# Attention's keys turned in one step, its units placed by other numbers, and the third gate group moved ahead of the branch projections

## The chip, the cores and the metric

The kernel runs on one core of one Trainium2 chip. The metric is the device time of one execution in microseconds (us). Before the change it was 1309.54 us, the median of 3 runs (1308.44 to 1310.19).

## The reference, cut to what matters

The program is a two-layer decoder trunk on 512 tokens of width 1024, all in float32. Each layer has a mixer (one wide input projection, a branch of windowed attention, a branch of mLSTM, gates, output projection) and a squared-ReLU MLP. The change is in the mixer:

```python
h = rmsnorm(x, norm_mix)
z = h @ w_in
q_a, k_a, v_a, q_m, k_m, v_m, o_m, if_m, gates = jnp.split(z, splits, axis=-1)
q_a = partial_rope(rmsnorm(q_a.reshape(B, S, 8, 64), att_q_norm), cos, sin)
k_a = partial_rope(rmsnorm(k_a.reshape(B, S, 2, 64), att_k_norm), cos, sin)
att = sliding_window_attention(q_a, k_a, v_a, att_sinks)      # blocks of 128, own and previous block
hm = mlstm_chunkwise(q_m, k_m, v_m, i_pre, f_pre)
hm = rmsnorm(hm, m_head_norm) * jax.nn.sigmoid(o_m)
g_a, g_m = jnp.split(gates, 2, axis=-1)
mixed = jax.nn.sigmoid(g_a) * (att @ w_att_branch) + jax.nn.sigmoid(g_m) * (hm @ w_m_branch)
x = x + mixed @ w_out
```

## The kernel before

**Matmuls.** TensorE (PE) works on float32 values that are split into a high part and a low rest (`wh`, `wl` for weights, `i` and others for activations), and every product is made of three matmuls (`mm3`, line 211). A *group* of the mixer is 512 output columns: 8 weight chunks of 128 x 512, each loaded by a DMA from SP's queue, split by ScalarE (ACT, line 192) and VectorE (DVE, line 193), and used by 4 x 3 = 12 matmuls of 128x512. These 12 matmuls are a *block*, the unit in which the program counts its own progress; a group is 8 blocks, 96 matmuls. A group's results leave PSUM by its own evictions.

**The order of the work.** `weave` (line 254) runs a list of such steps, the *fill*, each 0.25 blocks wide, and puts *side* steps between them when the fill has come to the block number that stands with them. Tile's scheduler then orders the instructions of each engine by priority, readiness by its own model and free buffers; the engines run their queues in order. The mixer's first weave makes attention's q, k, v and the gate logits. The second, in which the change lies, has nine groups as fill (line 865): mLSTM's q and k (blocks 0 to 8), gate groups 0 and 1 (to 24), mLSTM's v (to 32), the two halves of attention's branch projection (`a_steps`, to 48), gate group 2 (to 56), the o gate (to 64), gate group 3 (to 72).

**Attention in the second weave.** There are eight *units*, a unit being a block of 128 queries and one of the two key heads with its four query heads. Ahead of them stands the *rotation*: `k_vec(b)` and `q_vec(b)` (lines 585 and 602) normalise the keys or queries of token block b on DVE (line 570) and rotate 16 of the 64 dimensions by four GpSimd (POOL) instructions (lines 573 to 578). The *turn*: `k_tr(b)` and `q_tr(b)` transpose them on PE into an `aux` PSUM tile and evict that by ACT and DVE in pieces of 64 partitions (lines 597 to 600 for keys, 619 and 620 for queries). A unit then has `att_scores` twice (PE, then ACT line 642 and DVE line 643, which evict and mask), `att_softmax` (DVE lines 650 to 661, ACT line 656 for the exponentials), `att_probs` (PE transposes, ACT 204 and DVE 205 as eviction, POOL lines 675 and 677 as masks), and `att_out` (PE, then lines 689 to 697). Unit i is placed at block 7 + 1.65 i, its last step 5.65 blocks later.

**The aux tiles.** Everything on PE that is not a group's matmul writes an `aux` tile, of which there are two in PSUM. PE takes its instructions in order, so a PE instruction that needs an aux tile not yet evicted, or data not yet made, holds up the fill matmuls behind it.

**mLSTM in the second weave.** Its four heads start at block 28, 4.65 blocks apart: `m_decay`, four `m_weights` (exponentials on ACT lines 793 and 796, mask on POOL, product on DVE line 804) and four `m_out` (lines 806 to 817); `m_norm` stands at the end. Sigmoids of the gates (`sigmoid`, line 728) need another function table of ACT than the exponentials; `back` (line 733) loads the old one again. The gate groups 0 and 1 are gated after group 1, group 2 in the o gate's eviction (line 843).

## Time and profile before

| | |
|---|---|
| median of 3 runs | 1309.54 us |
| the profiled execution | 1309.28 us, its span 1307.5 us |
| PE busy | 1291.7 us, 99% of the span |
| DVE, ACT, POOL busy | 966.6, 780.2, 219.0 us |
| second weave, up to the first turn, layer 1 / layer 2 | from 46.5 / from 694.3 us |
| attention's units | 60.7 to 163.3 us / 708.5 to 811.2 us |
| mLSTM and after, to the weave's end | to 263 us / to 911 us |

The span is the time from the first to the last instruction; 1.78 us of the execution lie around it. All times in the trace count from the span's start. A row of the timeline has start, duration, engine, line, operation, output<-inputs and a count of merged instructions, and in brackets the idle time before it with what ended it. PE's matmuls are pipelined, so that a row's end is not the time at which the next may start. A row of the windows gives, for each engine, busy us and the number of instructions in that stretch.

### The profile page before, as it was taken

What the parts mean: (1) busy time and instruction counts of PE and PEld (TensorE: products, weight loads), DVE (VectorE), ACT (ScalarE), POOL (GpSimd) and SP (SyncE); (2) the same over time, 40 slices, a digit from 0 to 9 for tenths busy, and PEclk for the clock granted to TensorE, in tenths of its full rate; (3) what the DMA queues carried; (4) which work ended last, traced back from release to release, by engine and by line L of the source; (5) the groups of instructions that cost most, each with busy time, mean ns of one, the idle gap of its engine ahead of it and who ended that gap; (6) DMA issues with size and microseconds to landing.
All of it is one profiled execution on the core that took longest, in us unless ns stands there. A gap on an engine that the chain in (4) does not pass through costs nothing. (4 is left out here: it accounts for less than half of the span.)

```text
span 1307.5 us, 19591 instructions
## 1 busy us (share of the span) xinstructions
PE 1291.7 (99%) x7126; PEld 1110.3 (85%) x7126; DVE 966.6 (74%) x1507; ACT 780.2 (60%) x1393; POOL 219.0 (17%) x331
## 2 busy tenths in 40 slices
PE   9999999999999999999999999999999999999998
PEld 7877788888899989999888777888888999999987
DVE  4688765466589897979947887645766888979786
ACT  5568765544376666667544687554444676666663
POOL 4521301100011122110014113011000111212100
PEclk9999999999999999999999999999999999999999
DMA  5322236848298999787314221366492799997743
GB/s 154 110 73 74 57 88 155 186 118 227 69 206 203 264 186 235 173 184 203 100 35 121 65 73 57 111 155 169 121 265 50 194 230 248 179 260 152 187 139 136
DMA packets 139169, 196.52 MB, mean 150 GB/s; under 512 B 10424, under 2 KB 76576, under 8 KB 139072
## 3 DMA queue, kind: packets, MB, share of 16 engines
q1 hardware_dynamic: 93040, 135.88, 33.7%
q0 software_dynamic: 37568, 44.17, 21.9%
q10 hardware_dynamic: 8464, 15.21, 3.9%
q8 instruction: 56, 0.92, 0.3%
q14 instruction: 41, 0.34, 0.1%
HBM read 193.14 MB, written 31.46 MB: 172 GB/s over the span
## 5 line engine op out<-in xcount | busy, mean ns | idle before, releaser
L47 PE MATMUL mm<-i,wh 128*128 128x512 f32 (+1 forms) x1216 | 325.5, 354 | 0.0
L917 ACT ACTIVATE wh<-raw 128x1024 fp32r<-128x1024 f32 x218 | 229.3, 1056 | 134.5 <-PE mm L47 63.6
L921 DVE TENSOR_TENSOR wl<-raw,wh 128x1024 fp32r<-128x1024 f32 x218 | 264.1, 1220 | 60.1 <-ACT wh L917 58.5
L47 PEld LDWEIGHTS mm<-i,wh 128*128 128x128 f32 x1216 | 210.5, 190 | 26.4
L193 DVE TENSOR_TENSOR wl<-w,wh 128x512 fp32r<-128x512 f32 (+1 forms) x208 | 141.4, 682 | 122.5 <-ACT wh L192 114.2
L47 PE MATMUL mm<-i,wl 128*128 128x512 f32 (+1 forms) x608 | 214.1, 352 | 0.0
L192 ACT ACTIVATE wh<-w 128x512 fp32r<-128x512 f32 (+1 forms) x208 | 127.2, 612 | 138.5 <-PE mm L47 101.5
L47 PE MATMUL mm<-wh,uh 128*128 128x512 f32 x448 | 175.0, 391 | 0.0
L47 PE MATMUL mm<-wl,uh 128*128 128x512 f32 x448 | 174.8, 390 | 0.0
L47 PE MATMUL mm<-wh,ul 128*128 128x512 f32 x448 | 174.3, 389 | 0.0
L961 POOL DMA_DIRECT2D raw<-in_w_ff_dram x56 | 72.7, 1300 | 496.8 <-DVE wl L921 340.5
L47 PE MATMUL mm<-wh,i 128*128 128x512 f32 (+1 forms) x512 | 150.1, 371 | 0.0
L47 PEld LDWEIGHTS mm<-i,wl 128*128 128x128 f32 x608 | 115.1, 189 | 14.9
L47 PE MATMUL mm<-hs,wh 128*128 128x256 f32 x672 | 122.1, 283 | 0.0
L47 PEld LDWEIGHTS mm<-hs,wh 128*128 128x128 f32 x672 | 105.7, 192 | 1.1
L47 PEld LDWEIGHTS mm<-wh,i 128*128 128x128 f32 x512 | 92.1, 189 | 14.9 <-issue 0.7
L47 PEld LDWEIGHTS mm<-wh,ul 128*128 128x128 f32 x448 | 84.1, 188 | 17.9
L47 PEld LDWEIGHTS mm<-wh,uh 128*128 128x128 f32 x448 | 84.3, 188 | 16.4
L47 PEld LDWEIGHTS mm<-wl,uh 128*128 128x128 f32 x448 | 84.3, 188 | 15.9
L47 PE MATMUL mm<-hs,wl 128*128 128x256 f32 x336 | 95.1, 283 | 0.0
L47 PE MATMUL mm<-wl,i 128*128 128x512 f32 (+1 forms) x256 | 94.1, 368 | 0.0
L975 DVE SCALAR_TENSOR_TENSOR x<-mm,ninv,x 128x512 f32<-128x512 f32 x112 | 80.9, 744 | 10.3 <-PE mm L47 10.0
(246 smaller groups left out, 2186.7 us busy)
## 6 DMA issues: line engine op xcount, KB each, us to landing
raw<-in_w_ff_dram SPq DMA_DIRECT2D x124, 512.0 KB, 6.0
w<-in_w_in_dram SPq DMA_DIRECT2D x128, 256.0 KB, 2.7
raw<-in_w_ff_dram POOLq DMA_DIRECT2D x56, 512.0 KB, 8.0
sum<-in_w_ff_dram ACTq DMA_DIRECT2D x28, 512.0 KB, 5.4
raw<-sum SPq DMA_DIRECT2D x28, 512.0 KB, 4.3
sum<-in_w_ff_dram POOLq DMA_DIRECT2D x20, 512.0 KB, 6.3
w<-in_w_out_dram SPq DMA_DIRECT2D x32, 256.0 KB, 3.3
w<-in_w_att_branch_dram SPq DMA_DIRECT2D x16, 256.0 KB, 2.7
```

What stands on the lines that cost most here:

```text
L47: return nc.tensor.matmul(*args, **kw)
L192: last_wh[:] = sc.activation(wh[:, :off], raw[:, :off], AF.Copy), wh
L193: ve.tensor_tensor(wl[:, :off], raw[:, :off], f32(wh[:, :off]), op=ALU.subtract)
L917: last_wh[:] = sc.activation(hi, r, AF.Copy), hi[:, 0, :]
L921: ve.tensor_tensor(lo, r, f32(hi), op=ALU.subtract)
L961: nc.gpsimd.dma_start(r, w1_block(k, n, c0), accum_op=ALU.add)
L975: ve.scalar_tensor_tensor(xh[:, i, :], ps[i], norm.inv[:, 0 if sign > 0 else 1, b:b + 1], xh[:, i, :], op0=ALU.mult, op1=ALU.add)
```

## The change

In words:
- The keys of all four token blocks are normalised by one DVE instruction, rotated by four POOL instructions, and turned in one step: four transposes into one aux tile, evicted by eight pieces of 64x512 (two heads, four pieces each) where 32 pieces of 64x128 were. The query rotation of block 0 is placed ahead of the keys', and the keys' POOL instructions are told to follow it.
- The units start at block 4.75 (was 7) and stand 2.6 blocks apart (was 1.65), so that the last is placed at block 22.95 (was 18.55).
- mLSTM starts at block 31 (was 28).
- Gate group 2 (`s2`) comes ahead of the two branch projections in the fill, at blocks 32 to 40 (was 48 to 56).

```diff
-            r0 = 0 if nh == HQ else 8
-            ct, st = tabs[nh != HQ]
-            ve.tensor_tensor(xv, xv, rqk[:, b, r0:r0 + nh].unsqueeze(2).to_broadcast([P, nh, HD]), op=ALU.mult)
+            ct, st = tabs[0]
+            ve.tensor_tensor(xv, xv, rqk[:, b, 0:nh].unsqueeze(2).to_broadcast([P, nh, HD]), op=ALU.mult)
...
-            gp.tensor_tensor(xv[:, :, 0:ROPE], t1, t2, op=ALU.add)
+            turned.append(gp.tensor_tensor(xv[:, :, 0:ROPE], t1, t2, op=ALU.add))
...
-        def k_vec(b):
-            rope(kvi[:, b, 0:128].rearrange("p (h d) -> p h d", d=HD), b, HKV)
-
-        def k_tr(b):
-
-            ps = aux([P, P])
-            pe.transpose(ps, kvi[:, b, 0:128], ident)
+        def k_vec():
+
+            k4 = kvi[:, :, 0:128].rearrange("p b (h d) -> p b h d", d=HD)
+            ct, st = (t[:, l].unsqueeze(2) for t in tabs[1])
+            ve.tensor_tensor(k4, k4, rqk[:, :, 8:10].unsqueeze(3).to_broadcast([P, NB, HKV, HD]), op=ALU.mult)
+            t1, t2 = (sm([P, NB, HKV, ROPE], tag, 1) for tag in ("rp2", "rq2"))
+            with tc.issue_after(turned[0].ins):
+                gp.tensor_tensor(t1, k4[:, :, :, 0:ROPE], ct.to_broadcast([P, NB, HKV, ROPE]), op=ALU.mult)
...
+                gp.tensor_tensor(k4[:, :, :, 0:ROPE], t1, t2, op=ALU.add)
+
+        def k_tr():
+
+            ps = aux()
+            for b in range(NB):
+                pe.transpose(ps[:, b * P:(b + 1) * P], kvi[:, b, 0:128], ident)
             for h in range(HKV):
                 r = slice(64 * h, 64 * h + 64)
                 o = slice(64 - 64 * h, 128 - 64 * h)
-                c = slice((b + 1) * P, (b + 2) * P)
+                c = slice(P, (NB + 1) * P)
...
-        side = [(0, lambda: k_vec(0)), (0, lambda: q_vec(0)), (0, lambda: k_vec(1)), (0, lambda: q_vec(1)),
-                (7 - 1.25, lambda: k_tr(0)), (7 - 1.75, lambda: q_tr(0))]
+        first, apart = 4.75, 2.6
+        side = [(0, lambda: q_vec(0)), (0, k_vec), (0, lambda: q_vec(1)),
+                (first - 1.25, k_tr), (first - 1.75, lambda: q_tr(0))]
         for i, (b, kv) in enumerate(units):
-            at = 7 + 1.65 * i
+            at = first + apart * i
...
-                    side += [(at + 1, lambda b=b: k_vec(b + 2)), (at + 1, lambda b=b: q_vec(b + 2))]
-                side += [(at + 2 * 1.65 - 1.25, lambda b=b: k_tr(b + 1)), (at + 2 * 1.65 - 1.75, lambda b=b: q_tr(b + 1))]
+                    side.append((at + 1, lambda b=b: q_vec(b + 2)))
+                side.append((at + 2 * apart - 1.75, lambda b=b: q_tr(b + 1)))
...
-            at = 28 + 4.65 * h
+            at = 31 + 4.65 * h
...
-        side.append((28 + 4.65 * (MH + 1) + -0.55, m_norm))
+        side.append((31 + 4.65 * (MH + 1) + -0.55, m_norm))
...
         weave(feat_steps(acts, wcols(C_QM, 512), ev_qk) + s0 + s1 + tok_steps(acts, wcols(C_VM, 512), ev_v)
-              + a_steps(0, g0) + a_steps(1, g1) + s2 + tok_steps(acts, wcols(C_OM, 512), ev_o) + s3, side)
+              + s2 + a_steps(0, g0) + a_steps(1, g1) + tok_steps(acts, wcols(C_OM, 512), ev_o) + s3, side)
```

How the instructions stand on three engines, before and now. All three places are in layer 1; layer 2 has the same ones. Lines from 570 on are higher by 1 to 14 in the changed file.

**PE, the first turn of the second weave.** `mm<-i,wh` and `mm<-i,wl` are matmuls of mLSTM's q and k group (the number behind `wh` tells the weight chunk), `ident,a_193` the turn of query block 0, `ident,kvi` that of keys. Before, 63 of the weave's matmuls stand ahead of the query turn, the last of them here:

```order
L47 MATMUL mm_665<-i_153,wl_762 128x512
L51 MATMUL aux_768<-ident,a_193 128x128 x4
L47 MATMUL mm_666<-i_153,wh_761 128x512
L47 MATMUL mm_666<-i_154,wh_761 128x512
L47 MATMUL mm_666<-i_153,wl_762 128x512
L47 MATMUL mm_679<-i_153,wh_761 128x512
L47 MATMUL mm_679<-i_154,wh_761 128x512
L47 MATMUL mm_679<-i_153,wl_762 128x512
L51 MATMUL aux_789<-ident,kvi_197 128x128
```

Now 36 stand ahead of it:

```order
L47 MATMUL mm_673<-i_153,wl_701 128x512
L51 MATMUL aux_716<-ident,a_193 128x128 x4
L47 MATMUL mm_658<-i_153,wh_733 128x512
L47 MATMUL mm_658<-i_154,wh_733 128x512
L47 MATMUL mm_658<-i_153,wl_734 128x512
L47 MATMUL mm_659<-i_153,wh_733 128x512
L47 MATMUL mm_659<-i_154,wh_733 128x512
L47 MATMUL mm_659<-i_153,wl_734 128x512
L51 MATMUL aux_743<-ident,kvi_197 128x128 x4
```

The query turn moved from 5.25 to 3.0 blocks after the weave's start, and the key turn still follows it by six matmuls, but holds all four key blocks. Between the query turn and the first scores lie 21 matmuls before and 22 now. Further on in the same queue, 32 fill matmuls, a key turn and two aux tiles of scores lay between the turn of query block 1 and the first scores that read it; now 14 matmuls and one aux tile of scores lie there. For query block 3 it is now 7 matmuls and one aux tile of scores. The last `att_out` stands 31.1 blocks after the weave's start before and 30.1 now.

**POOL, the first rotations.** `a_193` and `a_194` are query blocks 0 and 1, `kvi_197` holds the keys, `rp` and `rq` are the two products and the last instruction of a set adds them. Before:

```order
L573 TENSOR_TENSOR rp_126_638<-kvi_197,ct_108 128x32
L574 TENSOR_TENSOR rq_127_639<-kvi_197,st_109 128x2x8
L576 TENSOR_TENSOR rq_127_639<-kvi_197,st_109 128x2x8
L578 TENSOR_TENSOR kvi_197<-rp_126_638,rq_127_639 128x2x16
L573 TENSOR_TENSOR rp_128_645<-a_193,ct_98 128x128
L574 TENSOR_TENSOR rq_129_646<-a_193,st_99 128x8x8
L576 TENSOR_TENSOR rq_129_646<-a_193,st_99 128x8x8
L573 TENSOR_TENSOR rp_130_652<-kvi_197,ct_108 128x32
L574 TENSOR_TENSOR rq_131_653<-kvi_197,st_109 128x2x8
L576 TENSOR_TENSOR rq_131_653<-kvi_197,st_109 128x2x8
L578 TENSOR_TENSOR a_193<-rp_128_645,rq_129_646 128x8x16
```

Now:

```order
L574 TENSOR_TENSOR rp_126_638<-a_193,ct_98 128x128
L575 TENSOR_TENSOR rq_127_639<-a_193,st_99 128x8x8
L577 TENSOR_TENSOR rq_127_639<-a_193,st_99 128x8x8
L579 TENSOR_TENSOR a_193<-rp_126_638,rq_127_639 128x8x16
L593 TENSOR_TENSOR rp_128_645<-kvi_197,ct_108 128x128
L594 TENSOR_TENSOR rq_129_646<-kvi_197,st_109 128x8x8
L596 TENSOR_TENSOR rq_129_646<-kvi_197,st_109 128x8x8
L598 TENSOR_TENSOR kvi_197<-rp_128_645,rq_129_646 128x4x2x16
L574 TENSOR_TENSOR rp_130_652<-a_194,ct_98 128x128
```

Query block 0 is rotated first instead of after key block 0 and around key block 1, and one set of four stands for all keys. On DVE the normalisation of query block 0 likewise stands ahead of the keys'.

**ACT, the sigmoids of gate group 2.** L730 is the sigmoid before and L743 the same now; `a_2574` to `a_2580` and `a_2175` to `a_2181` are the group's four tiles; L816/L830 and L817/L831 evict mLSTM's outputs, L807 is one of its exponentials, L799 the decay's eviction. Before, these stand behind the last exponential of the last head:

```order
L730 ACT_TABLE_LOAD
L730 ACTIVATE a_2574<-a_2574 128x512
L192 ACTIVATE wh_2679<-w_2677 128x512
L730 ACTIVATE a_2576<-a_2576 128x512
L730 ACTIVATE a_2578<-a_2578 128x512
L730 ACTIVATE a_2580<-a_2580 128x512
L816 ACTIVATE a_194<-aux_2565,dn_2568 128x128
```

Now they stand between the exponentials of heads 1 and 2:

```order
L743 ACTIVATE a_2179<-a_2179 128x512
L830 ACTIVATE a_196<-aux_2146,dn_2151 128x128
L799 ACTIVATE t_2199<-aux_2197 128x512
L831 ACTIVATE aux_2146,hss_629<-a_196 128x128
L807 ACT_TABLE_LOAD
L807 ACTIVATE t_2217<-t_2217,bias_594 128x128
L192 ACTIVATE wh_2340<-w_2338 128x512
L743 ACT_TABLE_LOAD
L743 ACTIVATE a_2181<-a_2181 128x512
L830 ACTIVATE a_193<-aux_2201,dn_2203 128x128
L192 ACTIVATE wh_2381<-w_2379 128x512
```

The four sigmoids are cut in two by an exponential, so that this stretch has four table loads (one ahead of the first sigmoid, the two shown, one ahead of the next exponential) where before it had one; the whole program has 12 table loads a layer where it had 9.

More of the change, by code (lines that the diff above doesn't have):

```diff
@@ L564, in mixer @@
         ve.tensor_tensor(v2[:, :, :, 1, :], v4, f32(v2[:, :, :, 0, :]), op=ALU.subtract)
+        turned = []
         def rope(xv, b, nh):
-            r0 = 0 if nh == HQ else 8
-            ct, st = tabs[nh != HQ]
-            ve.tensor_tensor(xv, xv, rqk[:, b, r0:r0 + nh].unsqueeze(2).to_broadcast([P, nh, HD]), op=ALU.mult)
+            ct, st = tabs[0]
+            ve.tensor_tensor(xv, xv, rqk[:, b, 0:nh].unsqueeze(2).to_broadcast([P, nh, HD]), op=ALU.mult)
             t1 = sm([P, nh, ROPE], f"rp{nh}", 1)
@@ L583, in mixer @@
         tri_i = tri_l.bitcast(I32)
-        def k_vec(b):
-            rope(kvi[:, b, 0:128].rearrange("p (h d) -> p h d", d=HD), b, HKV)
-        def k_tr(b):
-            ps = aux([P, P])
-            pe.transpose(ps, kvi[:, b, 0:128], ident)
+        def k_vec():
[5 more added lines that the diff above has]
+                gp.tensor_tensor(t1, k4[:, :, :, 0:ROPE], ct.to_broadcast([P, NB, HKV, ROPE]), op=ALU.mult)
+                gp.tensor_tensor(t2[:, :, :, 0:8], k4[:, :, :, 8:16],
+                                 st[:, :, :, 0:8].to_broadcast([P, NB, HKV, 8]), op=ALU.mult)
+                gp.tensor_tensor(t2[:, :, :, 8:16], k4[:, :, :, 0:8],
+                                 st[:, :, :, 8:16].to_broadcast([P, NB, HKV, 8]), op=ALU.mult)
+                gp.tensor_tensor(k4[:, :, :, 0:ROPE], t1, t2, op=ALU.add)
[3 more added lines that the diff above has]
+                pe.transpose(ps[:, b * P:(b + 1) * P], kvi[:, b, 0:128], ident)
             for h in range(HKV):
```

## The prediction

> **What bounds the kernel now.** I read the page's busy table first, then the windows, then the timeline.
>
> ```profile
> span 1307.5 us, 19591 instructions
> PE 1291.7 (99%) x7126; PEld 1110.3 (85%) x7126; DVE 966.6 (74%) x1507; ACT 780.2 (60%) x1393; POOL 219.0 (17%) x331
> ```
>
> PE is busy for 99% of the span, so the only thing that a change of order can give is PE's waits. The windows (stretch, length, then busy us and instructions of PE, PEld, DVE, ACT, POOL) say where they are: attention's units and the rest of the second weave, in layer 1 and in layer 2.
>
> ```profile
> 60.70:163.30 102.60, 97.73 (x475) 75.54 (x474) 84.47 (x200) 73.29 (x193) 28.77 (x54) 1.00 0.25 69
> 163.30:263.00 99.70, 99.70 (x492) 83.37 (x491) 54.25 (x145) 58.23 (x146) 13.03 (x28) 1.00 0.58 143
> 708.50:811.20 102.70, 97.80 (x476) 75.42 (x474) 84.38 (x199) 73.29 (x194) 28.74 (x54) 1.00 0.25 69
> ```
>
> Attention's stage shows 4.87 us without PE work in layer 1 and 4.90 in layer 2; the stage behind it shows none. DVE is busy for 82% and ACT for 71% of attention's stage, for 54% and 58% of the next. The idle time is not all of it, because a matmul's row outlasts the point at which the next could start. The real pace stands in PE's timeline:
>
> ```profile
> 46.47 0.61 PE L47 MATMUL mm<-i,wh 128*128 128x512 f32 x2
> ...
> 60.76 0.60 PE L51 MATMUL aux<-ident,a 128*128 128x128 f32 x4
> 61.11 0.71 PE L47 MATMUL mm<-i,wh 128*128 128x512 f32 x2
> ...
> 78.56 0.39 PE L47 MATMUL mm<-i,wh 128*128 128x512 f32 x1
> 80.36 0.30 PE L51 MATMUL aux<-ident,kvi 128*128 128x128 f32 x1 [1.41 <-DVE t L643]
> ...
> 82.10 0.62 PE L47 MATMUL mm<-i,wh 128*128 128x512 f32 x2
> 83.20 0.79 PE L47 MATMUL aux<-kT,t 128*128 128x256 f32 x4 [0.48 <-DVE t L643]
> ...
> 86.75 0.64 PE L47 MATMUL aux<-kT,t 128*128 128x256 f32 x4
> 87.23 0.39 PE L47 MATMUL mm<-i,wl 128*128 128x512 f32 x1
> ```
>
> From 46.47 to 60.76 lie the 63 matmuls that the order puts ahead of the query turn: 0.227 us each. Four score matmuls take 0.48 (86.75 to 87.23), four transposes 0.35 (60.76 to 61.11). By start to start, the wait at 78.56 is 80.36 - 78.56 - 0.227 = 1.57 us where the row shows 1.41, and that at 82.10 is 1.10 - 0.45 = 0.65 where it shows 0.48. So the stage's whole wait is its length less its work at this pace. The windows of the group tiles alone and two groups of the aux tiles give the work:
>
> ```profile
> 60.70:163.30 102.60, 77.81 (x311) 56.34 (x310) 7.69 (x12) 0.00 (x0) 1.00 0.25 69
> ...
> 60.70:163.30 102.60, 28.46 (x164) 20.85 (x164) 30.88 (x69) 26.12 (x59) 1.00 0.25 69
> ...
> L47 PE MATMUL aux<-t,v 128*128 128x512 f32 x28 | 8.6, 417 | 0.4 <-DVE t L205 0.2 <-POOL t L677 0.2
> L47 PE MATMUL aux<-kT,t 128*128 128x256 f32 x48 | 8.4, 297 | 1.1 <-DVE t L643 0.5 <-DVE t L526 0.3 <-DVE t L693 0.2
> ```
>
> 311 x 0.227 = 70.6; of the 164 aux matmuls 28 x 0.227 = 6.4, 48 x 0.12 = 5.8, and the other 88, mostly transposes, at 0.09 about 8: 91 us of work in 102.6. About 11 us are waits (9 to 14, as the 88 are priced at 0.12 or 0.07), in each layer. They are what the change can win. Nearly all that are named end with a DVE eviction of an aux tile: of two tiles one is not yet free, because DVE, four fifths busy, comes late.
>
> **The change part by part.** All per layer; the trace of layer 2 repeats layer 1.
>
> *Keys at once, less work off the path.* The evictions that go and the nearest rows for those that come (64x512, on ACT line 717, on DVE line 722):
>
> ```profile
> L598 ACT ACTIVATE kT<-aux,gc 64x128 fp32r<-64x128 f32 x8 | 2.9, 362 | 0.1
> L597 ACT ACTIVATE kT<-aux,gc 64x128 fp32r<-64x128 f32 x8 | 2.9, 360 | 1.3 <-DVE kT L599 0.7 <-PE aux L51 0.5
> L599 DVE SCALAR_TENSOR_TENSOR kT<-aux,gc,kT 64x128 fp32r<-64x128 f32 x8 | 2.8, 348 | 0.5 <-ACT kT L598 0.3
> L600 DVE CAST kT<-kT 64x128 fp32r<-64x128 f32 x8 | 2.4, 301 | 0.2
> ...
> L717 ACT ACTIVATE a<-a 64x512 fp32r<-64x512 f32 x8 | 5.0, 626 | 0.1
> L722 DVE TENSOR_TENSOR a<-a,a 64x512 fp32r<-64x512 f32 x4 | 3.1, 787 | 0.1
> ```
>
> ACT: 5.8 go, 4 x 0.63 = 2.5 come, 3.3 saved. DVE: 5.2 go, 4 x 0.30 (as short as the smaller cast) to 4 x 0.79 come, I take 2.6; saved 2.6 (2.0 to 4.0). DVE's four key normalisations become one, worth another half microsecond or so. PE does the same transposes. None of it is on the path: it counts through the waits.
>
> *First turn, 27 matmuls sooner.* PE now comes to the query turn at 46.47 + 36 x 0.227 = 54.64. What it waits for there is the rotation of query block 0:
>
> ```profile
> 53.00 0.29 DVE L570 TENSOR_TENSOR kvi<-kvi,rqk 128x128 f32<-128x128 f32 x1
> 53.21 0.69 DVE L570 TENSOR_TENSOR a<-a,rqk 128x512 f32<-128x512 f32 x1
> ...
> 53.37 0.64 POOL L573 TENSOR_TENSOR rp<-kvi,ct 128x32 f32<-128x32 f32 x1 [3.49 <-DVE kvi L570]
> ...
> 55.48 0.51 POOL L573 TENSOR_TENSOR rp<-a,ct 128x128 f32<-128x128 f32 x1
> ...
> 57.01 0.70 POOL L573 TENSOR_TENSOR rp<-kvi,ct 128x32 f32<-128x32 f32 x1
> ...
> 59.56 0.46 POOL L573 TENSOR_TENSOR rp<-a,ct 128x128 f32<-128x128 f32 x1
> ...
> 60.66 0.46 POOL L578 TENSOR_TENSOR a<-rp,rq 128x128 f32<-128x128 f32 x1
> ```
>
> DVE can normalise the queries at 53.00 in place of the keys, 0.69 us; POOL follows 0.08 later (53.29 to 53.37), at 53.77. A set of four took 59.56 to 61.12 = 1.56 us, and beside a busy DVE 57.01 - 55.48 + 0.46 = 1.99. So the queries are ready at 55.3 to 55.8: a new wait of 0.7 to 1.2 us, 1.0 taken (0.6 to 1.6). The keys follow on POOL, 56.9 to 57.8, and PE comes to them 0.35 + 6 x 0.227 = 1.7 later, at 57.0 to 57.5: 0.3 (0 to 1.0). The first scores stand 16 matmuls, 3.6 us, behind the key turn, and need one key head of ACT, DVE and a copy, 0.63 + 0.69 + 0.5 in line, with the query pieces between: 0.2 (0 to 0.8). Before the change all three were covered by 14.3 us of matmuls.
>
> *No key turn of block 1.* The two waits at 78.56 and 82.10 sit at that turn and behind it; 2.2 us go. What is late next is the turn of query blocks 1 and 3, whose scores now follow after 14 x 0.227 + 0.47 = 3.65 us and 7 x 0.227 + 0.48 = 2.1 us of PE work. They need the first two ACT and DVE pairs of the eviction:
>
> ```profile
> 61.44 0.47 ACT L619 ACTIVATE t<-aux,gc 64x256 fp32r<-64x256 f32 x1 [0.76 <-PE aux L51]
> ...
> 62.96 0.49 DVE L620 SCALAR_TENSOR_TENSOR t<-aux,gc,t 64x256 fp32r<-64x256 f32 x1 [0.54 <-ACT t L619]
> ...
> 72.70 0.47 ACT L619 ACTIVATE t<-aux,gc 64x256 fp32r<-64x256 f32 x1
> ...
> 78.02 0.49 DVE L620 SCALAR_TENSOR_TENSOR t<-aux,gc,t 64x256 fp32r<-64x256 f32 x1
> ```
>
> That took 2.0 us at the first turn and 5.8 at the second. Against 3.65 and 2.1 it is 0 to 2.2 plus 0 to 3.7. I take 0.8, nearer to the first turn, since DVE is less crowded.
>
> *Units spread.* The units now begin 2.25 blocks, 6.1 us, sooner and by the order end one block sooner, while DVE has some 3 us less: 81.5 us in about 105, 78% where it was 82%. Waits were about 11 us at 82% and none at 54%. In a straight line that takes 4/28 of the 8.8 us that are left, 1.3. But the backlog falls further than the load: the last output was placed at block 24.2 and stood at 31.1, almost 7 blocks overdue, and is now placed at 28.6 and stands at 30.1. Side steps that crowd each other for the two aux tiles are what PE runs into. I take twice the straight line, 2.6 (0 to 8.8). The end of the phase doesn't gain: there the last units' outputs stand as close behind their masks as before.
>
> *Group 2 first.* Three more table loads. A load shows in ACT's timeline:
>
> ```profile
> 110.55 1.28 ACT L656 ACT_TABLE_LOAD   x1
> 111.84 0.40 ACT L656 ACTIVATE t<-t,m 128x128 f32<-128x128 f32 x1
> ```
>
> 1.29 us, 3.9 in all, in a stage in which ACT was idle for 41 of 99.7 us. But two of them stand ahead of evictions that free an aux tile. I take 0.8 (0 to 2 x 1.29 = 2.6). The Trainium skill, ScalarE: Activation LUTs, section What ACT_TABLE_LOAD costs, puts a switch at 2.66 us with a drain; by that the three would be an estimated 8 us, and the term up to 5.3; the trace, where the next instruction starts 1.29 us after the load, disagrees. The group's fourth eviction must wait for a buffer that head 1 frees a block later; its PSUM bank is wanted again only after a whole group, so nothing. Its weight loads change places with the branch's on SP's queue, 256 KB either way: nothing.
>
> **The sum.** 1.0 + 0.3 + 0.2 + 0.8 + 0.8 - 2.2 - 2.6 = -1.7 us a layer, -3.4 in all. From the profiled execution's 1309.28 that is 1305.9; the median of the runs lay 0.26 above it, so 1306.1. Half of the range of each unknown makes 1303 to 1309 for this case.
>
> **The rivals.**
> *The waits go for good* (0.17). If three quarters of the 8.8 go, as the flat next stage suggests, and the query turns cost nothing: 2.3 - 2.2 - 6.6 = -6.5 a layer, 1296.5. For it: the waits follow DVE's load. Against it: 78% is still a heavy load.
> *The waits move* (0.18). The order's last `att_out` went from 31.1 to 30.1 blocks: the scheduler had long stretched the units to some 2.2 blocks each, whatever number stood there. Then nothing is spread, only the saved key work counts, and the new waits at the front eat the 2.2: 1309.5. For it: there are two aux tiles before and after. The Trainium skill, Perfetto Trace Analysis, section Identifying Performance Opportunities, says that a recurring bubble can mean too few buffers; the trace, whose waits end with evictions of aux tiles, agrees.
> *Slower: the query turns* (0.12). If both evictions take the 5.8 us of the second turn, PE waits 2.2 + 3.7 = 5.9: -1.7 - 0.8 + 5.9 = +3.4 a layer, 1316.3. It decides from 3.65 and 2.1 us after a turn on: are two query pieces out by then? The row at 72.70 speaks for it, that at 61.44 against.
> *Slower: the table loads* (0.08). If all 3.9 us reach PE, -1.7 + 3.1 = +1.4 a layer, 1312.3. It decides at the output evictions behind the second and fourth load: do they hold the aux tile that PE wants next? For it: the four sigmoids are cut in two, between exponentials. Against it: ACT's 41 idle us. The Trainium skill, ScalarE: Activation LUTs, section Rules for kernel authors, asks that all functions of one set be done before switching; no run here shows yet what breaking it costs.
>
> **How the numbers follow.** About 0.2% (2.6 us) is what a measurement of this kernel can tell from no change, that is 1306.9 to 1312.1. The forecast (0.45) lies below 1306.9 in three cases of four: 0.34 faster, 0.11 same. With the first rival and the tail of the second, faster is 0.54; same is 0.11 and 0.13 of the second rival, 0.24; slower 0.22. The range reaches past the forecast to most of the first rival and to the table loads: 1298 to 1313.
>
> **What the profile after would show.** Right: PE waits of about 1 us at the first query turn, on POOL's sum, in both layers; no wait at a key turn after that; idle PE in attention's stage down from 4.9 to some 3.5 us; DVE near 78% there. Wrong: waits of 2 us or more at scores behind a query turn, on line 633 of DVE; PE idle in the mLSTM stage, on ACT or the output evictions; or idle time in attention's stage as before.

## The result, and the profile after

The changed kernel takes 1317.30 us (median of 4 runs, 1316.22 to 1318.59), the kernel before, run beside it, 1309.28: a ratio of 1.0060, 95% interval 1.0048 to 1.0072. It is slower by 8 us, where 3.4 us less was forecast, and lies above the forecast's range. The profiled execution took 1318.59 us, 9.3 more than that of before, with a span of 1316.9 us against 1307.5.

The page's span and busy table come first.

```profile
span 1316.9 us, 19504 instructions
PE 1296.0 (98%) x7126; PEld 1111.5 (84%) x7126; DVE 959.0 (73%) x1477; ACT 780.0 (59%) x1375; POOL 215.5 (16%) x307
```

DVE's work fell by 7.6 us, as the saved key work said it would, and PE still lost 9.4 us of span. The windows of layer 1 show where (stretch, length, busy us of PE, PEld, DVE, ACT and POOL, then PE's granted clock).

```profile
54.10:57.00 2.90, 0.91 (x7) 0.52 (x6) 2.90 (x5) 0.63 (x1) 2.82 (x5) 1.00 0.19 30
57.00:61.00 4.00, 4.00 (x15) 3.00 (x14) 1.81 (x3) 1.89 (x4) 3.77 (x10) 0.60 0.35 109
...
60.70:163.30 102.60, 97.77 (x471) 75.75 (x469) 81.00 (x187) 68.75 (x180) 26.27 (x45) 1.00 0.25 67
```

The kernel before, in the first two of these stretches:

```profile
54.10:57.00 2.90, 2.90 (x15) 2.39 (x14) 2.90 (x7) 0.64 (x1) 2.82 (x6) 1.00 0.21 46
57.00:61.00 4.00, 4.00 (x21) 3.29 (x20) 2.18 (x4) 1.27 (x2) 3.92 (x10) 1.00 0.54 166
```

Attention's stage is as idle as before: 4.83 us without PE work where it was 4.87, though DVE's share fell to 79%. The two stretches ahead of it are new. Before, PE worked through all of that stretch; now it stands still for 2 us of 54.10 to 57.00, and from 57.00 to 61.00 it counts as busy all the time but counts 15 instructions instead of 21, with a mean granted clock of 0.60. PE's timeline has both.

```profile
54.10 0.39 PE L47 MATMUL mm<-i,wl 128*128 128x512 f32 x1
56.48 0.66 PE L51 MATMUL aux<-ident,a 128*128 128x128 f32 x4 [1.99 <-POOL a L579]
...
57.67 0.94 PE L47 MATMUL mm<-i,wh 128*128 128x512 f32 x2
...
58.89 1.12 PE L51 MATMUL aux<-ident,kvi 128*128 128x128 f32 x4
...
60.66 0.63 PE L47 MATMUL mm<-i,wl 128*128 128x512 f32 x1
61.09 0.68 PE L47 MATMUL mm<-i,wh 128*128 128x512 f32 x2
...
64.13 0.23 PE L47 MATMUL aux<-kT,t 128*128 128x128 f32 x1
...
64.89 0.55 PE L47 MATMUL aux<-kT,t 128*128 128x128 f32 x3 [0.26 <-DVE kT L613]
```

PE reaches the first query turn at 54.33 (54.10 + 0.227, the pace from start to start) and starts it at 56.48: a wait of 2.15 us on POOL's last rotation step. Four matmuls later, from 58.0 to 61.1, a matmul takes 0.43 us from start to start (60.66 to 61.09) instead of 0.227. Then the first scores wait once more. Layer 2 repeats it: a wait of 2.24 us behind the matmul at 706.89, slow matmuls from 709.8 to 712.5.

To compare kernels I add up, for each PE matmul, the time to the next one's start less an undisturbed pace (0.227 us for 512 columns and 0.12 for 256, as in the prediction, and 0.109 for 128), and cut each layer's second weave in two: the front, up to the first unit's last score matmul, and the rest, up to 263 and 907 us. Before, layer 1 lost 0.47 us in the front and 13.26 in the rest, layer 2 0.40 and 13.37. After, it is 4.67 and 13.61, 5.14 and 13.03. Of the 9.4 us of span 8.9 are in the fronts.

Why POOL was late stands in its own timeline and DVE's.

```profile
53.27 0.85 POOL L574 TENSOR_TENSOR rp<-a,ct 128x128 f32<-128x128 f32 x1 [3.89 <-DVE a L571]
54.08 0.77 POOL L575 TENSOR_TENSOR rq<-a,st 128x64 f32<-128x64 f32 x1
...
55.65 0.78 POOL L579 TENSOR_TENSOR a<-rp,rq 128x128 f32<-128x128 f32 x1
...
60.42 0.46 POOL L574 TENSOR_TENSOR rp<-a,ct 128x128 f32<-128x128 f32 x1
60.83 0.32 POOL L575 TENSOR_TENSOR rq<-a,st 128x64 f32<-128x64 f32 x1
...
61.51 0.46 POOL L579 TENSOR_TENSOR a<-rp,rq 128x128 f32<-128x128 f32 x1
```

```profile
52.50 0.69 DVE L571 TENSOR_TENSOR a<-a,rqk 128x512 f32<-128x512 f32 x1
53.11 0.69 DVE L590 TENSOR_TENSOR kvi<-kvi,rqk 128x512 f32<-128x512 f32 x1
53.71 0.96 DVE L571 TENSOR_TENSOR a<-a,rqk 128x512 f32<-128x512 f32 x1
54.59 0.80 DVE L193 TENSOR_TENSOR wl<-w,wh 128x512 fp32r<-128x512 f32 x1
55.32 1.66 DVE L571 TENSOR_TENSOR a<-a,rqk 128x512 f32<-128x512 f32 x2
```

Query block 0's set of four took 3.16 us (53.27 to 56.43); the same four instructions took 1.55 for a later query block (60.42 to 61.97). The first set ran beside DVE's normalisations of the keys and of the other three query blocks, which do not stop before 57. Both engines lengthen: DVE's normalisation goes from 0.69 to 0.96, POOL's short product from 0.32 to 0.77.

### The profile page after: what moved, and what is told of

It reads as the page before. It is cut to its first block, busy times and chain, and to the rows that moved or that the text cites. A ratio compares the mean times of both kernels' runs of the same rounds, so it can differ in the third digit from the quotient of the medians.

```text
span 1316.9 us, 19504 instructions
## 1 busy us (share of the span) xinstructions
PE 1296.0 (98%) x7126; PEld 1111.5 (84%) x7126; DVE 959.0 (73%) x1477; ACT 780.0 (59%) x1375; POOL 215.5 (16%) x307
## 5 line engine op out<-in xcount | busy, mean ns | idle before, releaser
L47 PE MATMUL mm<-i,wh 128*128 128x512 f32 (+1 forms) x1216 | 329.1, 356 | 0.0
L989 DVE SCALAR_TENSOR_TENSOR x<-mm,ninv,x 128x512 f32<-128x512 f32 x112 | 81.0, 745 | 10.2 <-PE mm L47 10.0
```

Of the source, the lines that this page charges most:

```text
L47: return nc.tensor.matmul(*args, **kw)
L989: ve.scalar_tensor_tensor(xh[:, i, :], ps[i], norm.inv[:, 0 if sign > 0 else 1, b:b + 1], xh[:, i, :], op0=ALU.mult, op1=ALU.add)
```

## The experiments

**Theory A**: the early first turn meets POOL's chain of rotations. PE waits for it, and the matmuls behind that wait run at half pace. **Theory B**, the rival with the prediction's own words: the loss comes from the units, from their spread and their query turns. **Theory C**: it comes from gate group 2 in front, with its table loads. A time below is a median, and its ratio is to the kernel before on the same chip, with the 95% interval; the kernel before had 1309.5 to 1309.8 there.

### The first turn, back in its place

```diff
-        first, apart = 4.75, 2.6
+        first, apart = 7, 2.6
```

> The changed kernel with its first query turn back at block 5.25 (units from block 7), still 2.6 apart. Theory A (the early first turn makes PE wait for POOL's rotation, and the matmuls behind that wait run at half clock): the 2.2 us wait and the half-clock stretch of about 1.3 us and the 0.5 us at the first scores go, in both layers, so 1317.3 - 2 x 4 = about 1309. Theory B (the loss comes from the spread units, crowded at their end, or from the query turns in the stage): still 1316 to 1318, or more, since the last units now end 2.25 blocks later, into the mLSTM stage. Theory C (the loss comes from gate group 2 and its table loads): still about 1317.

1309.36 us, 0.9997 (0.9987 to 1.0006). All of the loss goes with this one number, as A had it (it moves the units too; the next run moves the first turns alone), and what is left of the change is worth nothing that can be measured. The front is back at 0.81 and 0.85 us.

### The first turn alone, in the kernel before

```diff
-        side = [(0, lambda: k_vec(0)), (0, lambda: q_vec(0)), (0, lambda: k_vec(1)), (0, lambda: q_vec(1)),
-                (7 - 1.25, lambda: k_tr(0)), (7 - 1.75, lambda: q_tr(0))]
+        side = [(0, lambda: q_vec(0)), (0, lambda: k_vec(0)), (0, lambda: q_vec(1)), (0, lambda: k_vec(1)),
+                (4.75 - 1.25, lambda: k_tr(0)), (4.75 - 1.75, lambda: q_tr(0))]
```

> The kernel before with one thing changed: the queries of block 0 are rotated ahead of its keys, and the first query and key turns are placed at blocks 3.0 and 3.5, while the units stay at block 7 and 1.65 apart. Theory A: a wait of about 2 us at the first query turn in both layers and a half-clock stretch of 1 us or more behind it, so 1309.3 + 2 x 3.3 = about 1316 (the first scores are as late as before and cost nothing more). Theories B and C: nothing of the loss is here, 1309 to 1310.

1317.13 us (1314.42 to 1317.60), 1.0054 (1.0039 to 1.0069). The early turn alone makes the whole loss, with the units, the keys and the gate groups as they were. Its profiled execution was the 1314.42 one, and its two layers differ. PE's timeline at the two query turns, then the windows behind them:

```profile
55.60 0.66 PE L51 MATMUL aux<-ident,a 128*128 128x128 f32 x4 [2.06 <-POOL a L578]
56.01 0.71 PE L47 MATMUL mm<-i,wh 128*128 128x512 f32 x2
...
705.81 1.11 PE L51 MATMUL aux<-ident,a 128*128 128x128 f32 x4 [2.23 <-POOL a L578]
706.58 1.20 PE L47 MATMUL mm<-i,wh 128*128 128x512 f32 x2
```

```profile
55.60:60.00 4.40, 4.40 (x22) 3.68 (x23) 3.07 (x7) 3.00 (x7) 4.09 (x13) 1.00 0.28 88
...
705.80:710.00 4.20, 4.19 (x15) 3.49 (x16) 2.12 (x4) 1.45 (x4) 3.92 (x12) 0.62 0.30 87
```

After 2.06 us of idle PE by the row (2.23 from start to start) the clock stayed at 1.00, after 2.23 by the row (2.39) its mean over the next 4.2 us was 0.62. The front lost 2.58 us in the one layer and 4.13 in the other. The longer wait has 0.16 of the difference, so the low clock was worth about 1.4 us here, where nothing else waited behind it.

### Matmuls nobody uses in place of the wait

In front of the first query turn ten matmuls write the tile that the turn then overwrites.

```diff
             ps = aux()
+            if b == 0:
+                for _ in range(10):
+                    pe.matmul(ps, acts[0][0][:, 0:P], acts[0][0], start=True, stop=True)
             for j in range(4):
```

> The changed kernel with ten matmuls of 128x512 whose result nobody uses (2.3 us at 0.227 us each) ahead of the first query turn, so that PE works through the time in which it waits for the rotation. If the wait is what lowers the clock: the slow stretch goes, about 1.3 us a layer, and the wait's time is spent on the matmuls instead, so 1317.3 - 2.6 = about 1314.7, and 1.00 of granted clock from 57 to 61 us. If the clock falls for another reason: the slow stretch stays, and the time is 1317 to 1318. If the matmul's end is only recorded late and nothing is slow: 1317.

1316.86 us, 1.0056 (1.0041 to 1.0071): 0.4 less than the changed kernel, not 2.6.

```profile
54.73 2.43 PE L47 MATMUL aux<-i 128*128 128x512 f32 x10
57.01 0.66 PE L51 MATMUL aux<-ident,a 128*128 128x128 f32 x4
...
59.42 0.66 PE L51 MATMUL aux<-ident,kvi 128*128 128x128 f32 x4 [0.36 <-POOL kvi L598]
...
63.91 0.30 PE L47 MATMUL aux<-kT,t 128*128 128x128 f32 x1 [0.17 <-DVE t L636]
```

```profile
57.00:61.00 4.00, 3.64 (x20) 2.85 (x20) 2.34 (x4) 1.83 (x4) 3.76 (x9) 1.00 0.45 127
```

The clock did stay at 1.00, so a PE that is kept busy keeps it, as expected. But PE gets to the first scores hardly sooner: from its arrival at the turn it takes 9.2 us in layer 1 and 10.0 in layer 2, against 9.8 and 10.2 in the changed kernel. A faster PE only waits for the keys' turn instead, and at the scores again. So the low clock is a consequence that lies mostly beside the chain of POOL, ACT and DVE; the chain sets the front. My forecast for this run took the clock's price as additive, and that was wrong.

### Gate group 2, back behind the branch projections

```diff
-            at = 31 + 4.65 * h
+            at = 28 + 4.65 * h
...
-        side.append((31 + 4.65 * (MH + 1) + -0.55, m_norm))
+        side.append((28 + 4.65 * (MH + 1) + -0.55, m_norm))
...
-              + s2 + a_steps(0, g0) + a_steps(1, g1) + tok_steps(acts, wcols(C_OM, 512), ev_o) + s3, side)
+              + a_steps(0, g0) + a_steps(1, g1) + s2 + tok_steps(acts, wcols(C_OM, 512), ev_o) + s3, side)
```

> The changed kernel with gate group 2 back behind the branch projections and the mLSTM heads from block 28 again; units from 4.75, 2.6 apart, keys at once. Theory A: 1316 to 1317, less than 1 us of the loss is here. Theory C (the three more table loads and the sigmoids between the exponentials): about 1310 to 1313. Theory B: the last units now run into the mLSTM heads, which begin 3 blocks sooner, so 1318 or more.

1315.61 us, 1.0043 (1.0027 to 1.0060). The median is 1.7 below the changed kernel's, between what A and C expected, and the intervals overlap. The front hardly changed (4.76 and 4.50 us). One of the four executions had a granted clock of 1.000 over its whole span and still took 1314.46 us, 0.9 to 2.1 below the other three: here too the low clock is the smaller part of the loss. From 180 to 260 us PE loses 0.9 us instead of 1.7, so theory C has a small part of the truth.

### Keys at once, and nothing else

Keys turned as in the change; `first, apart = 7, 1.65`, and the group order and heads as before, by the lines above.

> The kernel before with the keys of all blocks normalised, rotated and turned at once, and nothing else changed: first query turn at block 5.25, units from 7, 1.65 apart, gate group 2 in its old place. If the two waits at the key turn of block 1 go for good, as the prediction's sum had it (2.2 us a layer): 1309.7 - 4.4 = about 1305. If they move to the next side step that wants an aux tile: 1308.5 to 1310. If the one key turn of four blocks is late at PE because POOL rotates four blocks in a row: 1311 or more.

1305.67 us (8 runs), 0.9970 (0.9960 to 0.9981). This kernel beats both. In the rest of each layer PE loses 2.0 and 2.2 us less (11.30 and 11.16 against 13.26 and 13.37), which is the 2.2 of the sum. But the gain is not where the sum had it. The key turn of block 1 is gone, and two waits of much the same size stand at the query turn and the scores around its old place. They end with the same eviction and mask of scores on DVE, line 656 (643 before):

```profile
73.77 0.63 PE L51 MATMUL aux<-ident,a 128*128 128x128 f32 x4 [0.99 <-DVE t L656]
...
82.07 1.20 PE L47 MATMUL aux<-kT,t 128*128 128x128 f32 x8 [1.28 <-DVE t L656]
```

From start to start they are 1.16 and 1.44 us, where the two waits of before were 1.57 and 0.65; layer 2 has 1.15 and 1.46. Up to 96.5 us this kernel loses as much in layer 1 as the one before, about 4.5 us each. What it gains stands at the end of the units: from 136.5 to 180.5 us it loses about 1.9 us instead of 4.2, and its last attention outputs start on PE at 156.96 instead of 162.52. Less work on DVE may be why attention ends sooner; no run tries that alone. So the time fits the first expectation and the place of the waits the second.

### The spread, at two distances

The kernel with keys at once alone, with one number changed.

```diff
-        first, apart = 7, 1.65
+        first, apart = 7, 2.2
```

> Keys at once, and units 2.2 blocks apart from block 7 on, gate group 2 in its old place and heads from block 28: the last output is placed at block 28.05. If spreading wins by itself (the prediction's 2.6 us a layer): about 5 below the kernel with keys at once alone, 1303 to 1305. If the scheduler stretches the units to some 2.2 blocks whatever number stands there: within 1 us of the kernel with keys at once alone.

1322.14 us, 1.0094 (1.0079 to 1.0109). Neither reading foresaw a loss of 16 us. With 1.9 in place of 2.2:

> Keys at once, first query turn at block 5.25, units 1.9 apart, heads from block 28 as before: a small step of the spread, the last output placed at block 25.95. With 2.2 apart the kernel took 1322.1, with 1.65 it took 1305.7. If the cost of spreading without moving the heads is the last units' meeting with the first head: little of it here, 1305 to 1308. If it grows evenly with the distance: 1305.7 + 16.4 x 0.25 / 0.55 = about 1313.

1310.91 us (10 runs), 1.0009 (0.9999 to 1.0018): 5 us above 1.65 apart, between my two guesses. Its largest wait stood in attention's stage and not at the heads: PE's turn of a unit's probabilities found its tile still held by ACT's eviction of a query piece (line 632).

```profile
82.56 0.63 PE L51 MATMUL aux<-ident,t 128*128 128x128 f32 x4 [2.40 <-ACT t L632]
```

This is a neighbour of the wait that the prediction's slower rival named. There the scores wait for the evicted queries, here another side step waits for the tile that the same eviction still holds. Which steps meet changes with the distance, so the times at 1.65, 1.9 and 2.2 apart need not follow a line; how far this explains them was not tried.

### The spread, with the heads three blocks later

```diff
-        first, apart = 7, 1.65
+        first, apart = 7, 2.6
...
-            at = 28 + 4.65 * h
+            at = 31 + 4.65 * h
...
-        side.append((28 + 4.65 * (MH + 1) + -0.55, m_norm))
+        side.append((31 + 4.65 * (MH + 1) + -0.55, m_norm))
```

> Keys at once, first query turn at block 5.25, units 2.6 apart, mLSTM heads from block 31, gate group 2 back behind the branch projections. Beside the kernel with keys at once alone the units are spread and the heads stand three blocks later. If the spread itself costs (adding up the runs so far: 1309.4 - 1.7): about 1307.7. If the spread is worth nothing either way: 1305 to 1306. If it wins what the prediction took: about 1301.

1317.47 us, 1.0061 (1.0046 to 1.0076), where the changed kernel's group order alone makes it 1309.36. PE's timeline shows what group 2 in front was hiding.

```profile
161.21 0.39 PE L47 MATMUL mm<-wh,i 128*128 128x512 f32 x1
164.38 1.08 PE L51 MATMUL aux<-ident,t 128*128 128x128 f32 x4 [2.78 <-DVE t L674]
166.35 2.50 PE L47 MATMUL mm<-u,wh 128*128 128x512 f32 x5 [0.88 <-ACT u L709]
```

The branch projections (`mm<-u`, line 709 writes the attention output they read) need every unit's output. Spread units end late, PE has come to the branch and waits 2.78 us for the last softmax (line 674) and 0.88 for the output, and the clock falls again behind it (0.91 over 140 to 180 us). The run at 2.2 apart waits 2.94 us at the same place, and from 160 to 180 and 820 to 840 us it loses 6.9 and 4.9 us more than with the keys alone: 12 of its 16.

### Group 2 in front, with the units close

```diff
-              + a_steps(0, g0) + a_steps(1, g1) + s2 + tok_steps(acts, wcols(C_OM, 512), ev_o) + s3, side)
+              + s2 + a_steps(0, g0) + a_steps(1, g1) + tok_steps(acts, wcols(C_OM, 512), ev_o) + s3, side)
```

To the kernel with keys at once alone, and the heads at 31.

> Keys at once, first query turn at block 5.25, units 1.65 apart as before; gate group 2 ahead of the branch projections and the mLSTM heads from block 31. Beside the kernel with keys at once alone (1305.7) only the group order differs. If the table loads and sigmoids between the exponentials cost what the changed kernel lost by them (1317.3 against 1315.6 with the group back): about 1307.4. If that price came from the spread units running late beside them: 1305 to 1306.

1307.12 us (9 runs), 0.9982 (0.9972 to 0.9992). The price of the group's place is there without any spread: 0.6 us more in the rest of each layer. Between 180 and 260 us, where the loads stand, PE loses 1.94 us instead of 1.01. By the medians it is 1.45 us, by the ratios 1.6.

### A first turn in between

```diff
-        first, apart = 4.75, 2.6
+        first, apart = 5.75, 2.6
```

> The changed kernel with the first query turn at block 4.0, so 12 matmuls or 2.7 us later than in the changed kernel and 18 matmuls sooner than before. PE comes to it at 57.4, and the rotation ended at 56.4: by theory A (the front's waits are POOL's chain of rotations) no wait there and no lowered clock, up to 0.5 us at the key turn (58.9 to 59.4 against 59.1) and 0.5 to 1 us at the first scores, so 1309.4 + 2 x 0.5 to 1.5 = 1310 to 1312. If the loss grows with every block that the units begin sooner (theory B): 1309.4 + 8 x 1.25 / 2.25 = about 1314.

1312.07 us (10 runs), 1.0021 (1.0012 to 1.0031), just past A's 1312 and below B's 1314. The query turn does not wait; the key turn waits 0.83 us by start to start, and the clock stays at 1.00. The front lost 1.78 and 1.58 us. A third of the loss for more than half of the way: a threshold more than a slope.

### Query block 0 rotated on DVE

Its four rotation instructions go to DVE, right behind its normalisation and ahead of the keys' and the other blocks'. `rope_ops` is the old body of `rope`.

```diff
+            with tc.issue_after(turned[0].ins) if b else tc.high_priority():
+                rope_ops(xv, b, nh)
...
+            en = ve if b == 0 else gp
-            gp.tensor_tensor(t1, xv[:, :, 0:ROPE], ct[:, l, b:b + 1, :].to_broadcast([P, nh, ROPE]), op=ALU.mult)
+            en.tensor_tensor(t1, xv[:, :, 0:ROPE], ct[:, l, b:b + 1, :].to_broadcast([P, nh, ROPE]), op=ALU.mult)
...
-            ve.tensor_tensor(k4, k4, rqk[:, :, 8:10].unsqueeze(3).to_broadcast([P, NB, HKV, HD]), op=ALU.mult)
+            with tc.issue_after(turned[0].ins):
+                ve.tensor_tensor(k4, k4, rqk[:, :, 8:10].unsqueeze(3).to_broadcast([P, NB, HKV, HD]), op=ALU.mult)
```

> The changed kernel, its first query turn still at block 3.0, with the rotation of query block 0 done on DVE, ahead of the other normalisations, instead of on POOL: four short instructions behind the query normalisation, so done at 52.5 + 0.7 + 4 x 0.25 = about 54.2, and PE comes at 54.6. POOL begins with the keys, at about 55.7, and ends them near 57.7. Theory A: no wait at the query turn, one of 1.0 to 1.7 us at the key turn (PE comes at 56.4), no lowered clock behind a wait this short, 0.3 at the first scores: about 2.3 us a layer less than the changed kernel, 1312 to 1313. If the front's loss is not POOL's rotation: 1317.

1317.14 us, 1.0058 (1.0043 to 1.0073): no gain. Half of the expectation held: the query turn started without a wait, at 54.11. The key turn, PE's next row below, did not hold to it, and the timelines of POOL and DVE say why.

```profile
58.54 0.65 PE L51 MATMUL aux<-ident,kvi 128*128 128x128 f32 x4 [2.38 <-POOL kvi L605]
```

```profile
55.33 0.84 POOL L600 TENSOR_TENSOR rp<-kvi,ct 128x128 f32<-128x128 f32 x1 [6.02 <-DVE kvi L597]
...
57.70 0.78 POOL L605 TENSOR_TENSOR kvi<-rp,rq 128x128 f32<-128x128 f32 x1
```

```profile
55.17 2.28 DVE L576 TENSOR_TENSOR a<-a,rqk 128x512 f32<-128x512 f32 x3
```

The keys' set took 3.15 us (55.33 to 58.48) beside DVE's three normalisations of query blocks 1 to 3, the set behind it 1.55 (58.45 to 60.00). So the wait went from the query turn to the key turn at its old length, and the clock fell behind it (a mean of 0.58 over 58.50 to 62.50).

### The same, with DVE quiet

The three normalisations now stand behind the key turn's first eviction on DVE.

```diff
-            with tc.issue_after(turned[0].ins) if b else tc.high_priority():
+            with tc.issue_after(turned[1].ins) if b else tc.high_priority():
                 rope_ops(xv, b, nh)
...
-                ve.scalar_tensor_tensor(kTl[r, h, c], ps[r, :], g, f32(kTh[r, h, c]), op0=ALU.mult, op1=ALU.subtract)
+                turned.append(ve.scalar_tensor_tensor(kTl[r, h, c], ps[r, :], g, f32(kTh[r, h, c]), op0=ALU.mult, op1=ALU.subtract))
...
-        side = [(0, lambda: q_vec(0)), (0, k_vec), (0, lambda: q_vec(1)),
+        side = [(0, lambda: q_vec(0)), (0, k_vec), (3.6, lambda: q_vec(1)),
```

> As the kernel with query block 0 rotated on DVE (1317.1), but the normalisations of query blocks 1 to 3 stand behind the key turn's first eviction on DVE, so that only one of DVE's long operations with two inputs runs beside POOL's rotation of the keys. If POOL was slow because of them (3.15 us for its set of four instead of 1.6): the set takes 1.6 to 2.2 us, the key turn waits about 1.0 to 1.5 instead of 2.4, the clock stays up behind so short a wait, and the time falls by 2 x (1.0 + 1.6) to about 1312. If POOL's set is as long without them: 1317.

1314.11 us (6 runs), 1.0035 (1.0023 to 1.0047). POOL's rows of the keys, then DVE's last operation with two inputs in SBUF beside them, then PE's key turn:

```profile
55.98 0.84 POOL L600 TENSOR_TENSOR rp<-kvi,ct 128x128 f32<-128x128 f32 x1 [6.03 <-DVE kvi L597]
56.79 0.31 POOL L601 TENSOR_TENSOR rq<-kvi,st 128x64 f32<-128x64 f32 x1
57.07 0.31 POOL L603 TENSOR_TENSOR rq<-kvi,st 128x64 f32<-128x64 f32 x1
57.45 0.45 POOL L605 TENSOR_TENSOR kvi<-rp,rq 128x128 f32<-128x128 f32 x1
```

```profile
55.82 0.68 DVE L193 TENSOR_TENSOR wl<-w,wh 128x512 fp32r<-128x512 f32 x1
```

```profile
57.96 0.66 PE L51 MATMUL aux<-ident,kvi 128*128 128x128 f32 x4 [1.16 <-POOL kvi L605]
```

Only the first of the four still ran beside DVE operations with two inputs in SBUF, and only it is long; the set took 1.92 us. The wait is halved, in layer 1 the clock behind it stays at 1.00, and the front loses 2.21 and 1.85 us instead of 4.59 and 4.40. I had expected 1312; 1.3 of the 2 us that are missing are in the rest of the weave (13.77 and 13.83 against 13.20 and 13.14), where DVE has the normalisations still to do. That DVE's work slows POOL's set for the keys, and by how much, is shown; for the set of query block 0 in the changed kernel, whose instructions have the same shapes, it is argued from this.

## Why the prediction was wrong

The experiments make a ladder from the kernel before to the changed one, one edit a step. Front and rest are PE's lost us in layer 1 and 2, by start to start, in the profiled executions.

| kernel | median us | ratio to before (95%) | front | rest |
|---|---|---|---|---|
| before | 1309.5 | 1 | 0.47, 0.40 | 13.26, 13.37 |
| + keys at once | 1305.67 | 0.9970 (0.9960 to 0.9981) | 0.79, 0.78 | 11.30, 11.16 |
| + group 2 first, heads from 31 | 1307.12 | 0.9982 (0.9972 to 0.9992) | 0.80, 0.77 | 11.91, 11.79 |
| + units 2.6 apart | 1309.36 | 0.9997 (0.9987 to 1.0006) | 0.81, 0.85 | 12.78, 12.67 |
| + units from 4.75 (the change) | 1317.30 | 1.0060 (1.0048 to 1.0072) | 4.67, 5.14 | 13.61, 13.03 |

The intervals of the middle steps overlap, so each of their prices rests on the profiles as much as on the times; the first and the last step stand by their times alone.

**The step that failed: "First turn, 27 matmuls sooner."** It was summed as 1.0 for the query turn, 0.3 for the key turn and 0.2 for the first scores, 1.5 us a layer, and 3.4 with the upper bound of all three; by the ladder's last step it costs 4 us a layer. Its place and its releaser were right, PE waits at the query turn on POOL's sum. Its size failed in three ways.
- POOL's set was priced at 1.56 to 1.99 us. The 1.56 is a set of the kernel before that met at most one of DVE's operations; the 1.99 adds its last step, 0.46, to three instructions that met DVE's normalisations in part (of the two short products one took 0.77 us, the other 0.36). Here all four met such operations, and the set took 3.16. The change puts query block 0's set exactly beside DVE's normalisations, which the diff moves together with it. POOL even began 0.5 us sooner than the step had said, so with a set of 1.99 the queries would have been ready at 55.26 and the wait 0.9 us. The quiet run shows that it is DVE that makes a set long: its keys' set took 1.92 us, against 3.15 beside the normalisations.
- The three waits were priced as if each stood alone. They are one chain: queries, then keys on the same engine, then the evictions. What it loses at the first link is lost at the last, whatever PE does between, as the unused matmuls showed.
- PE's clock was not in the sum at all. Behind the first wait of each layer it fell to 0.50 for 3.41 us. Where nothing else waited it was worth about 1.4 us, in one layer of the run with the early turn alone; in the changed kernel most of that lies beside the chain.

"Before the change all three were covered by 14.3 us of matmuls" was true and was the point: the change spends 6.1 us of that cover.

**The second step that failed: "Units spread", 2.6 us a layer gained.** It costs 0.9 a layer in the profiles. Part of it held: between 80 and 140 us PE loses 4.64 us instead of 6.90 with the spread units. But from 60 to 80 it loses 0.8 more, and from 140 to 180, where the last units now stand, 4.04 instead of 1.57. The prediction said that the end doesn't gain; it gives back all that the middle gains, and with it what keys at once had won there. The term was read from DVE's mean share and from how overdue the outputs were; where the last units stand the time is lost all the same. Which link of their chain holds PE there is shown for the kernel with the branch projections in their old place, and not for this one.

**Right in size, by luck: the key turn of block 1.** 2.2 us a layer were forecast, 2.0 and 2.2 measured, once the edit stood alone. But the two waits that were to go moved to the next steps that want an aux tile, as the rival had it by which the waits move. The gain came some 60 us later, where attention ends, of which the prediction said that it doesn't gain. That the two sizes agree is luck. In the changed kernel the gain is hidden by the steps that follow. The rival by which three quarters of the rest go for good falls: the kernel with keys at once alone, the fastest here, still loses 11.2 us and more in the rest of each layer.

**Right in size: group 2 first**, 0.8 us a layer forecast, 0.6 measured in the rest of the weave. Left out of the prediction was what it is good for: with the units spread and the branch projections in their old place, PE waits for the last unit's output, and the kernel takes 1317.5 instead of 1309.4. The rival by which all three table loads reach PE, 3.9 us a layer, falls with the 0.6; which of the loads stands behind it is not shown row by row.

**The rival of the query turns**, on the slower side, had the wrong place. It named 1316.3 us and the query turns of blocks 1 and 3, on line 633 of DVE. The time is near, the place is not: the changed kernel's waits on that line are 0.7 us in all, by the view of waits (us in total, times, longest). So the 0.8 us a layer that the sum had for these turns was too much as well.

```profile
PE aux L51 <- POOL a L579: 4.1, 2, 2.1
...
PE aux L47 <- DVE t L633: 0.7, 3, 0.3
```

Of the prediction's marks for "wrong", one came: attention's stage was as idle as before. Of those for "right", the place and the releaser of the first wait and DVE's share came.

**The clock, and POOL beside DVE.** The Trainium skill, TensorE: Matmul & The Clock Gate, section Part 1: The HAM clock gate, says that PE falls to half rate after an idle window of about 3.4 us, that these windows run freely, and that a busy window of that length brings the full rate back. The trace agrees with the half rate (0.43 against 0.227 us) and with windows of 3.41 us, whose place the last section works out; it differs on the start, since a window with 2.10 us of waits in it was enough, and the measurement decides. The Trainium skill, SBUF — State Buffer, section Who interferes with whom, says that a DVE instruction with two inputs in SBUF contends with a GpSimd instruction that reads SBUF. The trace agrees: POOL's short product takes 0.77 us beside such DVE operations and 0.31 or 0.32 without, and DVE's normalisation 0.96 instead of 0.69.

## What to carry to other kernels

When a step of a chain moves forward, price the chain up to the engine that bounds the kernel, with each link at its duration beside the work that moves with it, and ask how much cover is left at its end; a wait at the first link cannot be added to waits behind it. One edit at a time told here what the bundle hid: the first edit of the change was worth 3.9 us, and the rest of it lost three times as much. A term that comes out at its forecast size still has to be found at its place: the gain of the keys was not where the sum had put it. A reordering that looks like pure cost, as group 2 in front did, may be the cover of another.

## What the runs showed of the hardware that was not expected

PE's clock reacts to waits much shorter than I had thought possible, and not by their length alone. By start to start, over all the profiled executions, no wait of up to 2.05 us in the weaves lowered it. Of the six between 2.12 and 2.25, four brought a slow stretch and two did not; of the ten from 2.39 to 3.10, one did not (2.82, in layer 2 of the kernel with the units 2.2 apart).

What decides, in these traces, is where the wait falls. The granted clock is 0.50 for 3.41 us at a time (once for twice as long), and in each of the five executions with two falls they lie a whole number of such stretches apart: in the changed kernel the clock falls at 57.79 and at 709.74, 191 times 3.413 us later. So PE's waits can be counted in windows of this length, laid end to end from a fall. I count waits of 0.1 us and more, from 35 to 1290 us. Every window with 2.10 us or more of them, 13 in all, has the low clock behind it; no window at full clock with up to 2.04 us has it, and 14 of these have more than 1.5. The early turn alone shows one of each kind, every window followed by the next:

```profile
53.66:57.07 3.41, 1.47 (x9) 1.30 (x10) 3.32 (x8) 0.79 (x2) 3.41 (x8) 1.00 0.32 79
57.07:60.48 3.41, 3.41 (x17) 2.79 (x16) 2.01 (x6) 2.99 (x7) 3.10 (x14) 1.00 0.26 77
...
702.20:705.61 3.41, 1.38 (x7) 0.80 (x5) 3.41 (x8) 0.63 (x1) 3.34 (x7) 1.00 0.28 75
705.61:709.02 3.41, 3.21 (x10) 2.73 (x11) 2.31 (x4) 0.94 (x2) 3.25 (x10) 0.50 0.40 121
```

Of the 2.23 us wait in layer 1, 1.94 lie in the first of these windows; of the 2.39 in layer 2, 2.19 lie in the third. So the same program can have the low clock in one layer and not in the other, and in one execution and not in the next: the executions with gate group 2 moved back had mean granted clocks of 0.997 to 1.000. The spread of the runs of the early turn alone is not explained by this, since two of them at 0.999 took 1314.42 and 1317.12 us.

POOL and DVE slow each other by more than I allowed: POOL's set of four rotations took 1.55 us with no such DVE operation beside it, 1.92 with one of the four beside them, and 3.15 beside an unbroken run of them.
